# The second down projection of a hybrid decoder block: 16 of its 22 chunks as 2x2 blocks with seven block products

## The chip, the cores and the metric

The kernel runs on one core of a Trainium2 chip. TensorE (PE) multiplies, with its weight loads shown apart as PEld; VectorE (DVE), ScalarE (ACT) and GpSimd (POOL) do the element-wise work; SyncE (SP) and ACT issue DMAs. SBUF tiles have 128 partitions, results of PE land in eight PSUM banks of 128x512 float32. The metric is the device time of one execution in microseconds, as the median of several runs.

## The reference

A decoder block: a feed-forward layer, a mixer, and a second feed-forward layer, each between RMS norms, over 512 tokens and 1024 features, in float32. The part that matters here is the second feed-forward layer and its boundary:

```python
def swiglu(x, w_gu, w_down):                      # w_down: 2816 x 1024
    g, u = jnp.split(x @ w_gu, 2, axis=-1)
    return (jax.nn.silu(g) * u) @ w_down
...
        f = swiglu(rms_norm(h, ffn2_pre_g[l]), ffn2_w_gu[l], ffn2_w_down[l])
        h = h + MACARON_SCALE * rms_norm(f, ffn2_post_g[l])
```

With 128 rows to a chunk, the 2816 hidden features (ff) are 22 chunks.

## The kernel before

Every float32 operand is split into a high part, rounded to the matmul's input format (a cast on ACT), and a low part, the remainder (a subtraction on DVE). `mm3` (L129) makes a product of two split operands from three matmuls: high by high, high by low, low by high.

The stages follow one another: gate and up of layer 1 (`f1`), its down projection, the mixer, gate and up of layer 2 (`f2`), its down projection, and the last boundary (`b3`). A stage's gate and up matmuls are made in two ways: the first few chunks straight, the rest as pairs `k` = 0 to 17 in `paired` (L294), where a 2x2 block product is made with seven block multiplications (`product(1..7)`), 256 token columns moving, 12 matmuls each. Its order is written out by hand in `period(k)` under `tc.manual_schedule()`: products 1 and 2 of pair k, 5 of k-1, 6 and 7 of k, 3 and 4 of k-1, with preparation of the next pair's weights between. ACT copies a bank aside (`snap`), DVE adds (`add`), and `finish` makes the activations.

The down projection is `token_out` (L427). For each of the 22 chunks `wget` hands out one 128x1024 weight chunk: SP loads it as `wraw` (512 KB), `wsplit` (L96) casts on ACT (L100) and subtracts on DVE (L101). The activations `f2p` are split by chunk into `f2ph` and `f2pl` (L240, L241). Then for 4 token tiles of 128 and 2 halves of 512 output features one `mm3` each accumulates into the eight banks `f2o`: 24 matmuls of 128x512 per chunk, 528 in all. The last `TAILS[2]` = 5 chunks are kept back and multiplied token tile by token tile, so that tile after tile becomes ready. Outside `manual_schedule` a scheduler orders the instructions of each engine.

When a token tile is ready, `post_norm` (L199) takes its two banks: `Square` with a sum on ACT (L205), a scaled multiplication by the gain on DVE (L206), the mean on DVE (L209), the power -0.5 on POOL (L167), then on DVE the residual sum (L215) and out by two DMAs (L217).

Of the kernel before, what the change touches and what calls it, by code (L numbers as in the profile page):

```python
# [8 lines left out]
F32 = mybir.dt.float32  # L9
# [27 lines left out]

@with_exitstack
def hybrid_block_kernel(ctx, tc, x, xt, g1, w_first, gains, gu1, gs1, dn1, w_x, w_gate, w_q, w_k, w_v, w_gl, w_ga, w_pl, w_pa,
                        w_o, gu2, gs2, dn2, vecs, bd, sinks, rope, mask, out):  # L40
    nc = tc.nc
    V, A, G, PE, SP = nc.vector, nc.scalar, nc.gpsimd, nc.tensor, nc.sync

# [25 lines left out]
    for gu, dn in ((gu1, dn1), (gu2, dn2)):  # L69
        worder += [gu[j, i] for j in range(gu.shape[0]) for i in range(2)]  # L70
        caps.append(len(worder))
        worder += [dn[c] for c in range(KF)]
        if gu is gu1:
            worder += [w_x[c] for c in range(4)] + [w_k[i] for i in range(2)] + [w_v[i] for i in range(2)]
            worder += [w_x[c] for c in range(4, 8)] + [w_q[i] for i in range(4)]
            worder += [w_gate[c] for c in range(8)] + [w_q[i] for i in range(4, 8)]
            worder += [w[c] for c in range(8) for w in (w_gl, w_pl)]
            worder += [w[c] for c in range(8) for w in (w_ga, w_pa)]
            worder += [w_o[c] for c in range(8)]
# [163 lines left out]
    def gate_up(u, name, first, fast, rs=None):  # L243
        ps = []
        sp = []

        def split(c):
            if c % 4 == 0:
                sp.append((b8(f"{name}ph{c // 4}", [P, 4, T], F32R), b8(f"{name}pl{c // 4}", [P, 4, T], F32R)))
            split_chunk(ps[c // 4], *sp[-1], c % 4)  # L250

        def chunk(c):
            if c + 2 < KF and c >= 2:
                split(c + 2)
            return sp[c // 4]

        def tail(j, bg, bu):
            if j % 4 == 0:
                ps.append(b8(f"{name}p{j // 4}", [P, 4, T]))
# [8 lines left out]
            V.scalar_tensor_tensor(out=ps[-1][:, j % 4, :], in0=s, scalar=0.5, in1=bu, op0=ALU.mult, op1=ALU.mult)  # L268
# [20 lines left out]
        paired(fast(), name, ps)  # L289
        for c in range(4):  # L290
            split(c)
        return chunk

    def paired(fast, name, ps):  # L294
# [61 lines left out]
        def finish(k):  # L356
# [3 lines left out]
            if k % 2 == 0:  # L360
                d["ta"], d["tb"] = t2(f"{name}ta{k}"), t2(f"{name}tb{k}")
                ta, tb = d["ta"], d["tb"]
                A.activation(ta[:, lo_], a[:, lo_], AF.Tanh, scale=0.5)
                A.activation(ta[:, hi_], X, AF.Tanh, scale=0.5)
                A.activation(tb, b, AF.Tanh, scale=-0.5)
                for o, z in ((ta[:, lo_], a[:, lo_]), (ta[:, hi_], X), (tb, b)):
                    V.scalar_tensor_tensor(out=o, in0=o, scalar=1.0, in1=z, op0=ALU.add, op1=ALU.mult)
            else:
                ta, tb = st[k - 1]["ta"], st[k - 1]["tb"]
                if j % 4 == 0:  # L370
                    ps.append(b8(f"{name}p{j // 4}", [P, 4, T]))
                pa, pb = ps[-1][:, j % 4, :], ps[-1][:, j % 4 + 1, :]
# [9 lines left out]
        def period(k):  # L382
# [518 lines left out]
    chunk2 = gate_up(u3, "f2", first_four, lambda: (gs2, blocks(u3, mv3)))  # L901
    g_post, _ = gain_pair(5, 1, "g_b3")
    token_out(chunk2, KF, boundary(hs2, ov, g_post, None, None, 0.5, "b3"), "f2", TAILS[2])
# [5 lines left out]
def _layout(inputs):  # L909
# [44 lines left out]
    a["dn2"] = c(f["ffn2_w_down"].reshape(KF, P, D))  # L954
# [39 lines left out]
```

## Time and profile before

| | |
|---|---|
| median of 3 runs | 1159.97 us (1159.75 to 1160.45) |
| the profiled execution, first to last instruction (span) | 1158.4 us |
| median less span | 1.6 us |
| busy: PE, PEld, DVE, ACT, POOL | 98%, 87%, 69%, 46%, 5% of the span |
| second down projection, first to last matmul start | 1028.46 to 1150.93 us of the span |

The profiled execution has no time of its own beside its span; what lies around the span is taken as the median less the span. A matmul's row shows its own length, and matmuls overlap, so what one costs in a row of them is the distance between two starts (the pitch). The same holds for DVE and ACT, whose instructions in a row also start before the one before has ended.

### The profile page before, as it was taken

The numbers are of one execution on the slowest core, as the hardware profiler recorded it, in microseconds if no ns is written. First come the engines' busy times: TensorE is split into PE (matmuls) and PEld (weight loads), VectorE is DVE, ScalarE is ACT, GpSimd is POOL, SyncE is SP. The second block draws the span as 40 slices with busy tenths as digits, with TensorE's granted clock in tenths as the row PEclk, the third lists the DMA queues.
The fourth block names the chain that finished last, engine by engine and source line by source line (L and its number), as shares of the span: only waits on it lengthen the run. The fifth ranks groups of instructions, "written<-read, shape, count | busy, mean of one in ns | idle before, by whom it ended". The sixth has DMA issues, their size and how long they took to land.

```text
span 1158.4 us, 16623 instructions
## 1 busy us (share of the span) xinstructions
PE 1132.6 (98%) x6680; PEld 1008.4 (87%) x6680; DVE 804.2 (69%) x1182; ACT 537.3 (46%) x924; POOL 57.4 (5%) x58
## 2 busy tenths in 40 slices
PE   7979999999999999999999999999999999999997
PEld 6769999998888988887888888888999999998886
DVE  6598898984415887999877562546769898874303
ACT  7334555553313667566555341425435454553301
POOL 1000000000001010113121000000000000000000
PEclk9999999999999999999999999999999999999999
DMA  9113333284213453622822340624223333274011
GB/s 362 45 66 110 110 110 108 81 297 151 79 54 116 177 139 116 184 72 58 246 84 89 125 163 20 208 83 147 72 74 109 105 101 100 80 272 158 7 37 72
DMA packets 40604, 138.61 MB, mean 120 GB/s; under 512 B 4944, under 2 KB 5072, under 8 KB 39888
## 3 DMA queue, kind: packets, MB, share of 16 engines
q1 hardware_dynamic: 35920, 122.35, 32.4%
q10 hardware_dynamic: 4608, 15.21, 3.7%
q8 instruction: 52, 0.85, 0.3%
q14 instruction: 24, 0.20, 0.1%
HBM read 126.01 MB, written 11.53 MB: 119 GB/s over the span
## 4 chain that ended last, share of the span: by engine, by line
PE 87%; DVE 9%; ACT 2%; issue 2%; DMA 1%; POOL 0%; DVEq 0%; POOLq 0%; ACTq 0%
PE f1o L130 3%; PE f2o L130 3%; PE f1o L132 3%; PE f2o L132 3%; PE f1o L131 3%; PE f2o L131 3%; PE f2X L131 3%; PE f2X L132 3%; PE f2X L130 3%; PE f1X L130 3%; PE f1X L132 3%; PE f1X L131 3%; PE f1f L574 2%; PE f2Q L132 1%; PE f2Q L131 1%
## 5 line engine op out<-in xcount | busy, mean ns | idle before, releaser
L101 DVE TENSOR_TENSOR w<-wraw,w 128x1024 fp32r<-128x1024 f32 x128 | 155.7, 1244 | 67.0 <-ACT w L100 65.6
L100 ACT CAST w<-wraw 128x1024 fp32r<-128x1024 f32 x128 | 129.3, 1049 | 99.7 <-PE f1o L132 17.7
L130 PE MATMUL f1X<-u1m,f1W 128*128 128x256 f32 x256 | 73.1, 286 | 3.7 <-ACT f1sn L344 3.7
L132 PE MATMUL f1X<-u1m,f1W 128*128 128x256 f32 x256 | 73.2, 286 | 2.3 <-DVE f1W L324 2.3
L131 PE MATMUL f1X<-u1m,f1W 128*128 128x256 f32 x256 | 73.0, 285 | 0.0
L130 PE MATMUL f2o<-w,f2ph 128*128 128x512 f32 x176 | 68.6, 390 | 0.0
L130 PE MATMUL f1o<-w,f1ph 128*128 128x512 f32 x176 | 68.5, 390 | 0.0
L131 PE MATMUL f1o<-w,f1ph 128*128 128x512 f32 x176 | 68.5, 389 | 0.0
L131 PE MATMUL f2o<-w,f2ph 128*128 128x512 f32 x176 | 68.5, 389 | 0.0
L132 PE MATMUL f1o<-w,f1pl 128*128 128x512 f32 x176 | 67.0, 389 | 0.0
L132 PE MATMUL f2o<-w,f2pl 128*128 128x512 f32 x176 | 66.9, 389 | 0.0
L130 PEld LDWEIGHTS f1X<-u1m,f1W 128*128 128x128 f32 x256 | 49.6, 194 | 4.0 <-ACT f1sn L344 3.9
L132 PEld LDWEIGHTS f1X<-u1m,f1W 128*128 128x128 f32 x256 | 49.6, 194 | 2.6 <-DVE f1W L324 2.5
L131 PEld LDWEIGHTS f1X<-u1m,f1W 128*128 128x128 f32 x256 | 49.7, 194 | 0.1
L132 PE MATMUL f2X<-u3h,f2W 128*128 128x256 f32 x144 | 40.8, 283 | 0.0
L130 PE MATMUL f2X<-u3m,f2W 128*128 128x256 f32 x144 | 40.8, 283 | 0.0
L131 PE MATMUL f2X<-u3m,f2W 128*128 128x256 f32 x144 | 40.8, 283 | 0.0
L130 PE MATMUL f2Q<-u3m,f2W 128*128 128x256 f32 x144 | 40.8, 283 | 0.0
L131 PE MATMUL f2Q<-u3m,f2W 128*128 128x256 f32 x144 | 40.8, 283 | 0.0
L132 PE MATMUL f2Q<-u3m,f2W 128*128 128x256 f32 x144 | 40.8, 283 | 0.0
L131 PE MATMUL f2X<-u3l,f2W 128*128 128x256 f32 x144 | 40.8, 283 | 0.0
L132 PE MATMUL f2X<-u3m,f2W 128*128 128x256 f32 x144 | 40.7, 283 | 0.0
(722 smaller groups left out, 3519.9 us busy)
## 6 DMA issues: line engine op xcount, KB each, us to landing
wraw<-in_dn_dram SPq DMA_DIRECT2D x44, 512.0 KB, 4.7
f2L<-in_gs_dram SPq DMA_DIRECT2D x18, 512.0 KB, 3.6
f2R<-in_gs_dram SPq DMA_DIRECT2D x18, 512.0 KB, 4.4
wraw<-in_gu_dram SPq DMA_DIRECT2D x16, 512.0 KB, 5.8
f1L<-in_gs_dram SPq DMA_DIRECT2D x16, 512.0 KB, 3.6
f1R<-in_gs_dram SPq DMA_DIRECT2D x16, 512.0 KB, 4.4
wraw<-in_w_x_dram SPq DMA_DIRECT2D x8, 512.0 KB, 4.5
wraw<-in_w_q_dram SPq DMA_DIRECT2D x8, 512.0 KB, 4.4
```

Of the source, the lines that this page charges most:

```text
L100: A.copy(w[:, 0, :], raws[n])
L101: V.tensor_tensor(out=w[:, 1, :], in0=raws[n], in1=w[:, 0, :].bitcast(F32), op=ALU.subtract)
L130: PE.matmul(o, lhsT=ah, rhs=bh, start=start, stop=False, skip_group_check=reopen)
L131: PE.matmul(o, lhsT=ah, rhs=bl, start=False, stop=False, skip_group_check=reopen)
L132: PE.matmul(o, lhsT=al, rhs=bh, start=False, stop=stop, skip_group_check=reopen)
L574: PE.matmul(bs[i], lhsT=lw[:, i * P:(i + 1) * P], rhs=rx, start=k == 0 and n == 0, stop=k == KD - 1 and n == 2)
```

## The change

Chunks 0 to 15 of the second down projection become two groups (g = 0, 1) of 2x2 blocks. In a group the 512 tokens are two halves of 256, the ff features are two sets of four chunks (`GC`), and the 1024 outputs are two halves of 512. The four products of blocks of each output half become seven: the operands of a product are a block, or sums and differences of blocks, of the activations (token side) and of the weights. The weights of these chunks are laid out by quarter in a new input `ds2`.

A step is one product i, group g and half h of its contraction: 2 chunks x 2 token tiles x one `mm3`, 12 matmuls of 128x512. There are 7 x 2 x 2 = 28 steps, 336 matmuls, in the order of `PRODUCTS`. Chunks 16 to 21 are multiplied as before, 24 matmuls each, onto the same banks (144 matmuls). In all there are 480 matmuls in place of 528. `TAILS` for this stage goes from 5 to 4. The diff, cut to its core:

```diff
-TAILS = (6, 7, 5)
+TAILS = (6, 7, 4)
+GC = 4
+NS = 4 * GC
+LEAD = 3
+PRODUCTS = (1, 2, 5, 6, 3, 7, 4)
...
         for i in range(2):
-            A.activation(junk[:, cols[i]], banks[i], AF.Square, scale=1.0 / 32.0, accum_out=ms2[:, i:i + 1])
-            V.scalar_tensor_tensor(out=h[:, cols[i]], in0=banks[i], scalar=scale, in1=g[:, cols[i]],
+            z = banks[i]
+            if fix[i] is not None:
+                z = t2(f"{name}z{t}{i}")
+                V.tensor_tensor(out=z, in0=banks[i], in1=fix[i][0], op=fix[i][1])
+            A.activation(junk[:, cols[i]], z, AF.Square, scale=1.0 / 32.0, accum_out=ms2[:, i:i + 1])
+            V.scalar_tensor_tensor(out=h[:, cols[i]], in0=z, scalar=scale, in1=g[:, cols[i]],
                                    op0=ALU.mult, op1=ALU.mult)
...
         with tc.manual_schedule():
             for k in range(n):
                 period(k)
-        period(n)
-        add(n - 1, 21)
-        finish(n - 1)
+            if blocked is not None:
+                blocked.multiply(0)
+                blocked.prep(2)
+                product(5, n - 1, False)
...
+                blocked.multiply(1)
+                blocked.prep(3)
+                product(3, n - 1, False)
+                product(4, n - 1, False)
+                blocked.run(last, split_next)
...
+        def add_up(self, q):
...
+            if h == 0 and i in (5, 6, 3, 7):
...
+                V.tensor_tensor(out=o, in0=x0, in1=x1, op=ALU.subtract)
+            if i == 5:
+                z = self.raw[1, g, h]
+                V.tensor_tensor(out=z, in0=z, in1=self.raw[5, g, h], op=ALU.add)
+            if i == 7:
+                z = self.raw[5, g, h]
+                V.tensor_tensor(out=z, in0=z, in1=self.raw[3, g, h], op=ALU.add)
+
+        def prep(self, q):
+            self.load(q + 5)
+            self.add_up(q + 1)
...
+            w = b8(f"{self.name}w{i}{g}{h}", [P, 2, 2, 512], F32R)
+            A.copy(w[:, 0], z)
+            V.tensor_tensor(out=w[:, 1], in0=z, in1=w[:, 0].bitcast(F32), op=ALU.subtract)
+            self.w[i, g, h] = w
+            if i in (5, 6):
+                G.dma_start(first, self.ds[g, 3 if i == 5 else 2, h], accum_op=ALU.add)
...
+        def run(self, last, split_next):
+            for q in range(2, len(self.steps)):
+                if q == 3:
+                    last()
+                self.prep(q + LEAD - 1)
+                self.multiply(q)
+                for at_, key, of in ((6, "s1", "X"), (14, "s5", "Z"), (18, "s2", "X"), (26, "s3", "X")):
+                    if q == at_:
+                        self.snap(key, of)
+                if q == 20:
+                    open_loader()
+                if q in (23, 25, 26, 27):
+                    split_next()
```

`prep` makes a step's operands: for h = 0 the token operand `a` (cast on ACT, subtraction on DVE, both 128x1024), and for each h the weight operand `w` (the same). SP's `load` brings in 16 weight quarters of 512 KB; two more quarters per group and half are added to the one in SBUF by eight DMAs from POOL's queue with `accum_op`. `multiply(q)` is issued after the operands of the step two later. `multiply(0)` and `multiply(1)` stand between the last products of pair 17. The banks X, Y, Z and V, two each, hold the products; four copies (`snap`) keep values aside, and `post_norm` adds or subtracts one to each bank of a token tile.

On DVE, where the weights are prepared. Before, chunk weights `w` and the splits of the activations follow one another:

```order
L101 TENSOR_TENSOR w110_9940<-wraw110_9802,w110_9940 128x1024
L374 SCALAR_TENSOR_TENSOR f2p5_9854<-f2ta16_9806,f2X17_9686 128x256
L241 TENSOR_TENSOR f2pl1_9946<-f2p1_7944,f2ph1_9945 128x512 x2
L354 TENSOR_TENSOR f2cb17_9728<-f2Q17_9688,f2sn17_9725 128x256
L241 TENSOR_TENSOR f2pl1_9946<-f2p1_7944,f2ph1_9945 128x512 x2
L374 SCALAR_TENSOR_TENSOR f2p5_9854<-f2tb16_9807,f2cb17_9728 128x512
L101 TENSOR_TENSOR w111_9973<-wraw111_9877,w111_9973 128x1024
L101 TENSOR_TENSOR w112_10004<-wraw112_9914,w112_10004 128x1024
L101 TENSOR_TENSOR w113_10035<-wraw113_9943,w113_10035 128x1024
L101 TENSOR_TENSOR w114_10066<-wraw114_9976,w114_10066 128x1024
```

After, around the fifth product (`f2w21h`: weights of product 2, group 1; `f2b`: quarters as loaded; `f2sum`: differences of activations; `f2a`, `f2w`: low parts of a step's two operands):

```order
L535 TENSOR_TENSOR f2w210_9941<-f2b21_9774,f2w210_9941 128x1024
L505 TENSOR_TENSOR f2sum0_9958<-f2p0_7425,f2p1_7478 128x1024
L508 TENSOR_TENSOR f2b100_9682<-f2b100_9682,f2b50_9867 128x1024
L535 TENSOR_TENSOR f2w211_9961<-f2b21_9774,f2w211_9961 128x1024
L508 TENSOR_TENSOR f2b101_9684<-f2b101_9684,f2b50_9867 128x1024
L529 TENSOR_TENSOR f2a50_9977<-f2sum0_9958,f2a50_9977 128x1024
L535 TENSOR_TENSOR f2w500_9980<-f2b100_9682,f2w500_9980 128x1024
L505 TENSOR_TENSOR f2sum1_10000<-f2p8_8443,f2p9_8444 128x1024
L508 TENSOR_TENSOR f2b110_9686<-f2b110_9686,f2b51_9920 128x1024
L535 TENSOR_TENSOR f2w501_10003<-f2b101_9684,f2w501_10003 128x1024
L508 TENSOR_TENSOR f2b111_9688<-f2b111_9688,f2b51_9920 128x1024
L529 TENSOR_TENSOR f2a51_10020<-f2sum1_10000,f2a51_10020 128x1024
```

A quarter is added to another and an activation difference made before the low parts of the step: three instructions of 128x1024 for a step of product 5.

On ACT, in the period of the last pair (17). Before (`f2sn`, `f2sw`: banks copied aside; `f2W3`, `f2W4`: weights of pair 17; `w1xx`: the down projection's weights):

```order
L344 COPY f2sn17_9725<-f2X17_9686 128x256
L344 COPY f2sw16_9730<-f2X16_9577 128x256
L363 ACTIVATE f2ta16_9806<-f2ca16_9618 128x256
L344 COPY f2sn17_9725<-f2X17_9686 128x256
L323 CAST f2W317_9782<-f2L17_9436 128x1024
L323 CAST f2W417_9785<-f2N17_9569 128x512
L364 ACTIVATE f2ta16_9806<-f2X16_9577 128x256
L100 CAST w106_9794<-wraw106_9788 128x1024
L100 CAST w107_9799<-wraw107_9790 128x1024
```

After, casts of the first two steps and one of the third and their token operands stand among them:

```order
L524 ACTIVATE f2a10_9697<-f2p0_7425 128x1024
L534 CAST f2w100_9700<-f2b100_9682 128x1024
L365 COPY f2sn17_9742<-f2X17_9703 128x256
L365 COPY f2sw16_9747<-f2X16_9577 128x256
L534 CAST f2w101_9776<-f2b101_9684 128x1024
L365 COPY f2sn17_9742<-f2X17_9703 128x256
L344 CAST f2W317_9804<-f2L17_9436 128x1024
L344 CAST f2W417_9807<-f2N17_9569 128x512
L524 ACTIVATE f2a11_9825<-f2p8_8443 128x1024
L534 CAST f2w110_9828<-f2b110_9686 128x1024
L365 COPY f2sw17_9843<-f2X17_9703 128x256
```

The cast of `f2w100` now stands ahead of the copy `f2sn17`, which follows product 1 of pair 17.

On POOL, from the boundary ahead of layer 2 to the last one. Before:

```order
L167 TENSOR_TENSOR b2qpr3_7178<-b2qpe3_7176,mhalf_118 128x1
L167 TENSOR_TENSOR b2nr3_7186<-b2nme3_7184,mhalf_118 128x1
L167 TENSOR_TENSOR b3qpr0_10470<-b3qpe0_10468,mhalf_118 128x1
L167 TENSOR_TENSOR b3qpr1_10516<-b3qpe1_10514,mhalf_118 128x1
```

After, the eight accumulating DMAs stand between them, four for the fifth product's quarters and four for the sixth's:

```order
L172 TENSOR_TENSOR b2nr3_7186<-b2nme3_7184,mhalf_118 128x1
L538 DMA f2b100_9682<-in_ds2_dram 128x1024
L538 DMA f2b101_9684<-in_ds2_dram 128x1024
L538 DMA f2b110_9686<-in_ds2_dram 128x1024
L538 DMA f2b111_9688<-in_ds2_dram 128x1024
L538 DMA f2b100_9682<-in_ds2_dram 128x1024
L538 DMA f2b101_9684<-in_ds2_dram 128x1024
L538 DMA f2b110_9686<-in_ds2_dram 128x1024
L538 DMA f2b111_9688<-in_ds2_dram 128x1024
L172 TENSOR_TENSOR b3qpr0_10518<-b3qpe0_10516,mhalf_118 128x1
```

## Rows read from the trace of the kernel before

**Rows 1.** The page's first two parts: busy time in us, share of the span and number of instructions; and the granted clock of TensorE in 40 slices, in tenths.

```profile
span 1158.4 us, 16623 instructions
...
PE 1132.6 (98%) x6680; PEld 1008.4 (87%) x6680; DVE 804.2 (69%) x1182; ACT 537.3 (46%) x924; POOL 57.4 (5%) x58
...
PEclk9999999999999999999999999999999999999999
```

**Rows 2.** Busy time by stretch: eleven periods of pairs of gate and up of layer 2, up to the start of pair 17; the down projection ahead of its last tiles; its last tiles. Columns: us, then busy us and instructions of PE, PEld, DVE, ACT, POOL, then the granted clock, DMA share, GB/s.

```profile
906.60:1017.30 110.70, 110.70 (x925) 110.70 (x924) 99.77 (x154) 55.87 (x93) 0.00 (x0) 1.00 0.33 100
1040.00:1127.50 87.50, 87.50 (x388) 72.45 (x387) 29.74 (x33) 23.52 (x30) 0.00 (x0) 1.00 0.23 78
1127.50:1151.30 23.80, 23.80 (x106) 19.38 (x104) 9.45 (x16) 4.83 (x14) 1.65 (x3) 1.00 0.18 67
```

**Rows 3.** Timeline of PE near the end of the down projection: start, length, line, operation. The second row is the 27th matmul after the first, and the last of the kernel.

```profile
1144.81 0.39 PE L132 MATMUL f2o<-w,f2pl 128*128 128x512 f32 x1
...
1150.93 0.39 PE L132 MATMUL f2o<-w,f2pl 128*128 128x512 f32 x1
```

**Rows 4.** The stretch of the down projection again, only instructions that touch `f2o`: PE, PEld, DVE, ACT with their numbers.

```profile
1028.30:1151.30 123.00, 120.13 (x528) 98.97 (x528) 4.84 (x7) 4.83 (x14) 1.00 0.29 103
```

**Rows 5.** Timeline of PE: the first matmul of pair 16 and of pair 17 (84 matmuls apart).

```profile
1006.70 0.28 PE L130 MATMUL f2X<-u3h,f2W 128*128 128x256 f32 x1
...
1016.78 0.28 PE L130 MATMUL f2X<-u3h,f2W 128*128 128x256 f32 x1
```

**Rows 6.** Timeline of DVE, instructions that follow each other without a wait: 256, 1024, 1024 and 512 columns, and later 512 and three of 1024 in one row.

```profile
922.04 0.41 DVE L352 TENSOR_TENSOR f2cb<-f2Q,f2sw 128x256 f32<-128x256 f32 x1
922.38 1.21 DVE L324 TENSOR_TENSOR f2W<-f2M,f2W 128x1024 fp32r<-128x1024 f32 x1
923.51 1.22 DVE L324 TENSOR_TENSOR f2W<-f2L,f2W 128x1024 fp32r<-128x1024 f32 x1
924.64 0.68 DVE L324 TENSOR_TENSOR f2W<-f2N,f2W 128x512 fp32r<-128x512 f32 x1
...
1040.06 0.68 DVE L374 SCALAR_TENSOR_TENSOR f2p<-f2tb,f2cb 128x512 f32<-128x512 f32 x1
1040.66 3.49 DVE L101 TENSOR_TENSOR w<-wraw,w 128x1024 fp32r<-128x1024 f32 x3
```

**Rows 7.** Timeline of ACT: the copy aside of pair 17's first product, with the idle time before it, and three casts of 128x1024 in one row.

```profile
1018.42 0.37 ACT L344 COPY f2sn<-f2X 128x256 f32<-128x256 f32 x1 [3.92 <-PE f2X L132]
...
1038.75 2.95 ACT L100 CAST w<-wraw 128x1024 fp32r<-128x1024 f32 x3
```

**Rows 8.** Timeline of the end, after the last matmul.

```profile
1151.36 0.60 ACT L205 ACTIVATE b3qsq<-f2o 128x512 f32<-128x512 f32 x1 [2.71 <-PE f2o L132]
1151.85 0.19 ACT L205 ACTIVATION_READ_ACCUMULATOR b3qsq<-f2o 128x1 f32 x1
1152.08 0.69 DVE L206 SCALAR_TENSOR_TENSOR b3rh<-f2o,g_b 128x512 f32<-128x512 f32 x1 [2.71 <-ACT b3qsq L205]
1152.69 0.20 DVE L209 TENSOR_SCALAR b3qpe<-b3qps 128x1 f32<-128x1 f32 x1
...
1153.62 1.42 DVE L215 SCALAR_TENSOR_TENSOR b3rh<-b3rh,b3qpr 128x512 f32<-128x512 f32 x2 [0.73 <-POOL b3qpr L167]
```

**Rows 9.** Timeline of POOL and DVE, two places in the mixer where both work, and one where POOL does not.

```profile
549.30 1.29 POOL L710 TENSOR_TENSOR q2m<-q2m,q2m 128x512 f32<-128x512 f32 x1
549.50 1.11 DVE L770 TENSOR_TENSOR at13ss<-at13ss,at13e 128x4 f32<-128x4 f32 x1 [0.93 <-ACT at13s L768]
...
593.15 1.90 POOL L772 TENSOR_TENSOR at21s<-at21s,at21ss 128x1024 f32<-128x1024 f32 x1 [3.46 <-issue]
593.43 2.70 DVE L101 TENSOR_TENSOR w<-wraw,w 128x1024 fp32r<-128x1024 f32 x1 [0.41 <-ACT w L100]
...
617.49 0.16 DVE L770 TENSOR_TENSOR at22ss<-at22ss,at22e 128x4 f32<-128x4 f32 x1 [0.42 <-ACT at22s L768]
```

**Rows 10.** DMAs of 512 KB: SP's first issues for the down projection (time of the first, eight issues in the row); all 22 of them with the time of the issuing instruction and the min/median/max to landing; and the loads of x at the kernel's start, KB each and median us to landing.

```profile
1005.39 23.59 SPq L93 DMA_DIRECT2D wraw<-in_dn_dram  x8
...
L93 SPq DMA_DIRECT2D wraw<-in_dn_dram x22: 327/328/606, 1005.4 to 1069.3; - x22
DMA to landing us min/median/max: 3.3/4.5/7.6
...
x<-in_x_dram SPq DMA_DIRECT2D x4, 512.0 KB, 8.4
```

More of the change, by code (lines that the diff above doesn't have):

```diff
@@ L39, in hybrid_block_kernel @@
 def hybrid_block_kernel(ctx, tc, x, xt, g1, w_first, gains, gu1, gs1, dn1, w_x, w_gate, w_q, w_k, w_v, w_gl, w_ga, w_pl, w_pa,
-                        w_o, gu2, gs2, dn2, vecs, bd, sinks, rope, mask, out):
+                        w_o, gu2, gs2, dn2, ds2, vecs, bd, sinks, rope, mask, out):
     nc = tc.nc
@@ L71, in hybrid_block_kernel @@
         caps.append(len(worder))
-        worder += [dn[c] for c in range(KF)]
+        worder += [dn[c] for c in range(dn.shape[0])]
         if gu is gu1:
@@ L197, in to_features, with post_norm @@
                 A.copy(raw[half][:, :, ts_], bv)
-    def post_norm(banks, t, g, rh, scale, name, dst=None):
+    def post_norm(banks, fix, t, g, rh, scale, name, dst=None):
         ms2 = sm(f"{name}ps{t}", 2)
@@ L241, in split_chunk, with gate_up, pw @@
         V.tensor_tensor(out=pl[:, i, :], in0=p[:, i, :], in1=ph[:, i, :].bitcast(F32), op=ALU.subtract)
-    def gate_up(u, name, first, fast, rs=None):
-        ps = []
+    def gate_up(u, name, first, fast, rs=None, ds=None):
+        ps = {}
         sp = []
+        base = NS if ds is not None else 0
+        def pw(j):
+            if j < base:
+                key, slot, n = (j // (2 * GC), j % 2), j // 2 % GC, GC
+            else:
+                key, slot, n = (j - base) // 4, (j - base) % 4, 4
+            if key not in ps:
+                ps[key] = b8(f"{name}p{j}", [P, n, T])
+            return ps[key][:, slot, :]
         def split(c):
-            if c % 4 == 0:
-                sp.append((b8(f"{name}ph{c // 4}", [P, 4, T], F32R), b8(f"{name}pl{c // 4}", [P, 4, T], F32R)))
-            split_chunk(ps[c // 4], *sp[-1], c % 4)
+            i = c - base
+            if i % 4 == 0:
+                sp.append((b8(f"{name}ph{i // 4}", [P, 4, T], F32R), b8(f"{name}pl{i // 4}", [P, 4, T], F32R)))
+            split_chunk(ps[i // 4], *sp[-1], i % 4)
         def chunk(c):
-            if c + 2 < KF and c >= 2:
+            if c + 2 < KF and c >= base + 2:
                 split(c + 2)
-            return sp[c // 4]
+            return sp[(c - base) // 4]
         def tail(j, bg, bu):
-            if j % 4 == 0:
-                ps.append(b8(f"{name}p{j // 4}", [P, 4, T]))
             s = t2(f"{name}s{j}")
@@ L267, in tail @@
             V.scalar_tensor_tensor(out=s, in0=s, scalar=1.0, in1=bg, op0=ALU.add, op1=ALU.mult)
-            V.scalar_tensor_tensor(out=ps[-1][:, j % 4, :], in0=s, scalar=0.5, in1=bu, op0=ALU.mult, op1=ALU.mult)
+            V.scalar_tensor_tensor(out=pw(j), in0=s, scalar=0.5, in1=bu, op0=ALU.mult, op1=ALU.mult)
         bs = []
@@ L288, in gate_up, with paired @@
             tick()
[L289 to L294, printed above, removed]
+        blocked = None if ds is None else Blocked(name, ps, ds)
+        ahead = iter(range(base, base + 4))
+        paired(fast(), name, pw, blocked, lambda: split(next(ahead)))
+        if blocked is None:
+            for c in range(4):
+                split(c)
+        return chunk, blocked
+    def paired(fast, name, pw, blocked, split_next):
         src, mv = fast
@@ L389, in period @@
                 parts(d, 1)
+            elif blocked is not None:
+                blocked.prep(0)
             if c:
@@ L406, in period @@
                     parts(d, 2)
+                elif blocked is not None:
+                    blocked.prep(1)
                 snap(k, "s2")
@@ L413, in period, with last @@
                 parts(k, 4)
-            if k == n - 1:
-                wcap[0] = caps[caps.index(wcap[0]) + 1]
-                wload(wpos[0] + RAHEAD)
+            if k == n - 1 and blocked is None:
+                open_loader()
                 wsplit(wpos[0] + AHEAD)
+            if blocked is not None and k == n - 2:
+                for q in range(5):
+                    blocked.load(q)
             load(k + 3)
+        def last():
+            add(n - 1, 21)
+            finish(n - 1)
         with tc.manual_schedule():
@@ L428, in token_out, with open_loader @@
+    def open_loader():
+        wcap[0] = caps[caps.index(wcap[0]) + 1]
+        wload(wpos[0] + RAHEAD)
+    def token_out(chunk, n, epilogue, name, tail_n, blocked=None):
         banks = {}
+        base = NS if blocked is not None else 0
         def block(t, c, w, half):
@@ L432, in block @@
             ts_ = slice(t * P, (t + 1) * P)
+            opened = None if blocked is None else blocked.opened(t, half)
             if (t, half) not in banks:
-                banks[t, half] = bank(f"{name}o{t}{half}")
+                banks[t, half] = bank(f"{name}o{t}{half}") if opened is None else opened
             ns = slice(half * 512, (half + 1) * 512)
-            mm3(banks[t, half], ph[:, c % 4, ts_], pl[:, c % 4, ts_], w[0][:, ns], w[1][:, ns], c == 0, c == n - 1)
+            mm3(banks[t, half], ph[:, (c - base) % 4, ts_], pl[:, (c - base) % 4, ts_], w[0][:, ns], w[1][:, ns],
+                c == base and opened is None, c == n - 1, opened is not None)
         chunks = {}
         tail = []
-        for c in range(n):
+        for c in range(base, n):
             w = wget()
@@ L453, in token_out @@
                     block(t, c, w, half)
-            start(epilogue(t, (banks[t, 0], banks[t, 1])))
+            fix = [None, None] if blocked is None else [blocked.correction(t, half) for half in range(2)]
+            start(epilogue(t, (banks[t, 0], banks[t, 1]), fix))
             tick()
@@ L468, in boundary, with epilogue @@
         residual()
-        def epilogue(t, banks):
+        def epilogue(t, banks, fix):
             residual()
-            h = post_norm(banks, t, g_post, rhs[t], scale, f"{name}q", dst[t] if g_pre is None else None)
+            h = post_norm(banks, fix, t, g_post, rhs[t], scale, f"{name}q", dst[t] if g_pre is None else None)
             if g_pre is None:
@@ L899, in hybrid_block_kernel @@
                                                   lambda: moving(raw3, "u3", mv3)), "wo", TAILS[1])
[L901 removed]
+    chunk2, blocked2 = gate_up(u3, "f2", first_four, lambda: (gs2, blocks(u3, mv3)), None, ds2)
     g_post, _ = gain_pair(5, 1, "g_b3")
[L903 removed]
+    token_out(chunk2, KF, boundary(hs2, ov, g_post, None, None, 0.5, "b3"), "f2", TAILS[2], blocked2)
 _VECS = ["conv_b", "lru_b_a", "lru_b_x", "lru_lambda"]
@@ L953, in _layout, with quarters @@
     a["gu2"], a["gs2"] = gu(f["ffn2_w_gu"])[:JSTD["f2"]], pairs_of(f["ffn2_w_gu"], JSTD["f2"])
-    a["dn2"] = c(f["ffn2_w_down"].reshape(KF, P, D))
+    a["dn2"] = c(f["ffn2_w_down"].reshape(KF, P, D)[NS:])
+    def quarters(w):
+        b = w[:NS * P].reshape(2, 2, 2, 2, P, 2, 512)
+        return c(b.transpose(0, 5, 3, 1, 4, 2, 6).reshape(2, 2, 2, 2, P, 1024))
+    q = quarters(f["ffn2_w_down"])
+    a["ds2"] = c(np.stack([q[:, 0, 0], q[:, 1, 0], q[:, 0, 1], q[:, 1, 1]], 1))
     vec = [f["conv_w"][i] for i in range(4)] + [f[n] for n in _VECS]
```

87 lines of the change are left out of this document (82 added, 5 removed).

## The prediction

> **What bounds the kernel now.** I read the page's first parts, then busy time by stretch, then timelines at both ends of the changed stage. PE is busy for 98% of the span, at nine tenths of its full clock or more in each slice [rows 1]. Over the down projection ahead of its last tiles PE is busy for 87.50 of 87.50 us, DVE for 29.74, ACT for 23.52 [rows 2]: PE alone sets the pace there, and the other two have room. In the pairs before it DVE is nearly full too, 99.77 of 110.70 us [rows 2]; a preparation that reaches back into the last pair finds little room there. A matmul costs its pitch: from 1144.81 to 1150.93 are 27 of them, 0.2267 us each [rows 3]. A 256-column matmul costs 0.12 us, from 84 in 10.08 us [rows 5].
>
> The stage closes to the microsecond. Pair 17 ends its own period at 1016.78 + 10.08 = 1026.86. Its products 5, 3 and 4 are 36 matmuls, 4.32 us; 528 matmuls [rows 4] are 119.70; together 1150.88. The last one really starts at 1150.93 and so ends its turn at 1151.16 [rows 3]: 0.28 us of gaps in 124 us.
>
> **Matmuls.** 336 + 144 = 480 in place of 528, of the same shape. 48 x 0.2267 = **10.88 us** less, if PE still never waits. Nothing hides this, as PE is the bound; what hides a wait must be shown step by step.
>
> **When PE needs what.** multiply(0) runs from 1026.86, a step takes 12 x 0.2267 = 2.72 us, product 5 of the pair 1.44, multiply(1) follows, then 2.88 us of products 3 and 4. Step q from 2 on starts at S(q) = 1036.62 + 2.72 x (q - 2): S(10) = 1058.4, S(12) = 1063.8, S(14) = 1069.3, S(15) = 1072.0, S(22) = 1091.0, S(27) = 1104.6.
>
> **DVE in the blocks.** By the code the operations of 128x1024 per product are 6 for products 1, 2 and 4 (2 low parts of `a`, 4 of `w`), 8 for 6 and 3 (two differences more), 12 for 5 and 7 (four weight additions more): 58. One costs 1.13 us of pitch (922.38, 923.51, 924.64; and three in 3.49 less an overlap), 512 columns 0.60, 256 columns 0.34 [rows 6]. 58 x 1.135 = 65.8 us against 28 x 2.72 = 76.2 of PE: enough on the whole, but not in products 5 and 7, with 13.6 us of DVE beside 10.9 of PE. So the lead must last. DVE last waits for the pair's product 5: that ends at 1031.0, ACT's copy takes 0.37 like the one in [rows 7], so DVE goes on at about 1031.7. From there to the low part of step 10 the order has 18 operations of 1024 columns (20.4 us) and 3.5 us of small ones of the last pair (seven of 256 columns, two of 512): 1055.6. PE wants it at 1058.4: a lead of 2.8 us, the smallest. To step 22 are 28 more, 31.8 us: 1087.4 against 1091.0, lead 3.6. Cost: **0**; the cover is DVE's lead, and whatever takes more than 2.8 us from DVE before step 10, or 3.6 before step 22, shows on PE one for one.
>
> **ACT.** 42 casts at 0.98 (three in 2.95) [rows 7] are 41 us of 76, and eight copies of banks at about 0.6. Each copy of a bank stands behind casts that run with DVE's work, two to six steps ahead of the matmul that overwrites it; its cover is the same lead. 0.
>
> **DMA.** SP loads 16 + 6 pieces of 512 KB where it loaded 22; eight more come over POOL's queue: 30 against 22, in a stretch where the DMA engines are 23% busy [rows 2]. 0 for SP's. For the eight accumulating ones the trace has no row. A plain 512 KB takes 3.3 to 7.6 us to landing, 8.4 in the crowd at the start [rows 10]. The tightest is the third: it can start when step 10's low part is made (1055.6) and must have landed a cast (1.0) and a subtraction (1.22) before S(14): 1069.3 - 2.3 - 1055.6 = 11.4 us. I take the middle of the nearest row, 4.5 us, so 0. Bounds: 3.3 (0 as well) and twice the slowest, 15.2, an estimate for a transfer that also reads its target: 3.8 us.
> The Trainium skill ("DMA: Bandwidth & Descriptors", section "Anatomy of one DMA — SWDGE (gpsimd) path") fits a GpSimd-issued DMA as 2.0 us plus bytes over 436e3, an estimate of 3.2 us for 512 KB; no run here shows an accumulating one, and by that figure the sum would be the same.
>
> **The end.** The last bank is first corrected by DVE (0.69, the length of its neighbour in [rows 8]), then ACT squares it while DVE multiplies. Before, Square began at 1151.36, its sum ended at 1152.04, DVE's multiplication ran after it and the mean began at 1152.69 [rows 8]: 1.33 us. Now 0.69 + about 0.1 to pass it on + 0.68 for Square and its sum = 1.5, DVE beside it: **+0.15**, bounds -0.1 (the pass free, DVE's mean at once) and +0.69 (nothing overlaps). Per tile DVE has two corrections (1.3), two multiplications (1.3), the mean and the last sum (1.42): 4.2 us, under 24 x 0.2267 = 5.44 that a tile now takes on PE, so earlier tiles are not late.
>
> **Sum.** -10.88 + 0.15 = -10.73. The span goes from 1158.4 to 1147.7; the profiled run's time has 1.6 us around the span, taken as unchanged, so against the median 1159.97 the forecast is **1149.2**. Own range 1148.2 (no gap left, the low end bound) to 1150.5 (the high bound and half a microsecond of waits at the hand-over of stages).
>
> **Rivals.**
> *B, POOL holds DVE.* While POOL worked on SBUF, a DVE subtraction of 1024 columns took 2.70 us, not 1.22, and a tiny one 1.11, not 0.16 [rows 9]: 1.48 and 0.95 lost. DVE's operations in the blocks have two SBUF inputs, and POOL issues eight DMAs beside them. If making each one holds DVE as long, DVE loses 7.6 to 11.8 us before step 22, of which 3.6 is covered: 1153.2 to 1157.4. Against: POOL's rows are computations on SBUF data, and DMA issues carry none. Chance 0.12.
> The Trainium skill ("SBUF — State Buffer", section "Who interferes with whom") says that a VectorE instruction with two SBUF inputs contends with a GpSimd instruction that reads SBUF, which these rows bear out with 1.48 us; it infers that building DMA descriptors needs the write interface only, by which this rival would fall away.
> *C, the accumulates land late.* At 15.2 us each, side by side: 15.2 - 11.4 = 3.8 us: 1153.0. For: they read and write their target. Against: the engines are 23% busy. 0.09.
> *D, they go one after another, and it is slower.* Each waits for the one before, R apiece. The fourth, started in turn from step 8's low part (1055.6 less six operations = 1048.8), must land by S(15) - 2.3 = 1069.7: loss 4R - 20.9; the eighth by S(27) - 2.3 = 1102.3: 8R - 53.5. At R = 7.6 the larger is 9.5 (1158.7); at 8.4 it is 13.7 (1162.9). Slower than before from R = 8.0 on. For: one queue, and a crowd did take 8.4 [rows 10]. Against: SP's issues, one queue too, land in 4.5 while several are under way. 0.09.
> *E, the hand-over in the last pair.* The cast of `f2w100` now stands on ACT ahead of the copy of pair 17's first product, which had to wait 3.92 us for PE at 1018.42 [rows 7]. The cast needs quarter 100, whose load stands where SP's first issue stood, 1005.39 [rows 10]; the copy must be done by 1021.2 (product 6 overwrites the bank). Even 8.4 us would do; a late buffer on top would cost PE 1 to 3 us: 1150 to 1153. 0.06.
> That the change doesn't do what it says is excluded: the order on PE has 48 rows fewer.
>
> **Numbers.** Forecast 0.64, B 0.12, C 0.09, D 0.09, E 0.06. A measurement can tell 0.2%, 2.3 us, from no change. Faster (under 1157.65): all but D and a little of B, 0.89. Within: the lower part of D and the top of B, 0.04. Slower (over 1162.3): the rest of D, 0.07. The range leaves out D and the upper half of B, about 0.15, and a little below: 1148.0 to 1155.5.
>
> **What would show it.** Right: matmuls on the blocks' banks in one unbroken row of 0.2267 us from 1027 to 1140, the last about 11.2 us earlier; DVE's step-10 low part some 3 us ahead of PE. B: DVE rows of 1024 columns over 1.3 us beside POOL's DMA rows. C or D: PE idle before products 6 or 4, with a POOL DMA as releaser, and its time to landing over 11 us, or growing from one to the next. E: PE idle near 1021. Wrong in the main term: a pitch of the block matmuls other than 0.2267.

## The result, and the profile after

The changed kernel takes 1150.09 us (median of 4 runs, 1149.67 to 1151.21), the kernel before beside it 1159.86; the ratio is 0.9918, 95% interval 0.9904 to 0.9932. The forecast was 1149.2. The span of the profiled execution goes from 1158.4 to 1147.9 us; the forecast's was 1147.7.

The page's parts that answer to [rows 1]:

```profile
span 1147.9 us, 16623 instructions
...
PE 1121.6 (98%) x6632; PEld 999.0 (87%) x6632; DVE 847.0 (74%) x1216; ACT 558.2 (49%) x942; POOL 64.4 (6%) x66
...
PEclk9999999999999999999999999999999999999999
```

There are 48 matmuls fewer (6632 against 6680), the share of PE is unchanged, and DVE's busy time is 43 us up. Two stretches of the changed stage, the blocks from step 2 on and the six straight chunks; columns as in [rows 2]:

```profile
1036.60:1107.30 70.70, 70.31 (x309) 57.63 (x308) 67.12 (x64) 45.79 (x53) 7.11 (x8) 1.00 0.63 176
1107.30:1140.30 33.00, 33.00 (x147) 27.35 (x146) 16.88 (x27) 4.79 (x13) 1.66 (x3) 1.00 0.13 48
```

In the blocks PE is busy for 70.31 of 70.70 us, and DVE for 67.12, 95%: it has become nearly as tight as PE. Before, DVE was busy for a third of the time there, and the DMA engines' share was 0.23, which is 0.63 now [rows 2]. One place shows that it was too tight, in the timeline of PE (start, length, line, operation, and in brackets the idle time before and what ended it); the last row is the kernel's last matmul:

```profile
1090.98 0.39 PE L135 MATMUL f2X<-f2w,f2a 128*128 128x512 f32 x1
1091.75 0.50 PE L136 MATMUL f2X<-f2w,f2a 128*128 128x512 f32 x1 [0.39 <-DVE f2w L535]
1092.09 0.39 PE L137 MATMUL f2X<-f2w,f2a 128*128 128x512 f32 x1
...
1140.40 0.39 PE L137 MATMUL f2X<-w,f2pl 128*128 128x512 f32 x1
```

Between 1090.98 and 1091.75 PE misses 0.54 us over its pitch, and the next start is late by 0.11 too: step 22 waited for a DVE instruction. With 0.19 at step 21 (its rows are not shown), PE loses 0.85 us by these rows. There is no other gap in the blocks. Why DVE was late stands in its own timeline, the low parts of steps 13, 14 and 15 and, in the last row, of steps 22 and 23:

```profile
1062.30 1.23 DVE L535 TENSOR_TENSOR f2w<-f2b,f2w 128x1024 fp32r<-128x1024 f32 x1 [0.65 <-ACT f2w L534]
...
1066.19 1.22 DVE L535 TENSOR_TENSOR f2w<-f2b,f2w 128x1024 fp32r<-128x1024 f32 x1 [1.53 <-ACT f2w L534]
...
1069.89 1.23 DVE L535 TENSOR_TENSOR f2w<-f2b,f2w 128x1024 fp32r<-128x1024 f32 x1 [1.33 <-ACT f2w L534]
...
1090.48 2.35 DVE L535 TENSOR_TENSOR f2w<-f2b,f2w 128x1024 fp32r<-128x1024 f32 x2
```

DVE stood idle 0.65 + 1.53 + 1.33 = 3.51 us, each time until ACT had cast a weight quarter. ACT in turn waited for a DMA. The view of the line with the accumulating DMAs (operation, number, length of the issue; who waited for them; time to landing):

```profile
L538 POOL DMA_DIRECT2D f2b<-in_ds_dram x8: 863/866/1033, 1049.7 to 1071.4; - x8
...
  ACT f2w L534: 6.7, 3
...
DMA to landing us min/median/max: 5.7/9.8/10.5
```

They landed in 5.7 to 10.5 us, 9.8 in the median, where I had taken 4.5.

A ledger from the start of multiply(0) (1026.52 in the trace after) to the start of the last matmul: if PE never waits it is 36 x 0.12 + 479 x 0.2267 = 112.91 us; the changed kernel took 113.88. The kernel before took 124.07 by the same measure (1026.86 to 1150.93). So 11.2 us were to be had, its 0.28 us of gaps among them, and 10.2 came. The last pair began 0.34 us earlier in this execution (1016.44 against 1016.78 in [rows 5]); multiply(0) starts between 1025.64 and 1028.33 us in the traces that follow, so below everything is measured from there. Each kernel of the experiments but the last two was run once.

### The profile page after: what moved, and what is told of

It is laid out like the page before. It is cut to its first block, busy times and chain, and to the rows that moved or that the text cites. A ratio compares the mean times of both kernels' runs of the same rounds, so it can differ in the third digit from the quotient of the medians.

```text
span 1147.9 us, 16623 instructions
## 1 busy us (share of the span) xinstructions
PE 1121.6 (98%) x6632; PEld 999.0 (87%) x6632; DVE 847.0 (74%) x1216; ACT 558.2 (49%) x942; POOL 64.4 (6%) x66
## 4 chain that ended last, share of the span: by engine, by line
PE 85%; DVE 10%; ACT 2%; issue 2%; DMA 1%; POOL 0%; DVEq 0%; POOLq 0%; ACTq 0%
PE f2X L136 4%; PE f2X L137 4%; PE f2X L135 4%; PE f1o L135 3%; PE f1o L137 3%; PE f1o L136 3%; PE f1X L135 3%; PE f1X L137 3%; PE f1X L136 3%; PE f1f L736 2%; PE f2Q L137 2%; PE f2Q L136 2%; PE f2Q L135 2%; DVE w L106 1%; PE f1Q L135 1%
## 5 line engine op out<-in xcount | busy, mean ns | idle before, releaser
L106 DVE TENSOR_TENSOR w<-wraw,w 128x1024 fp32r<-128x1024 f32 x112 | 136.4, 1248 | 44.8 <-ACT w L105 43.4
L105 ACT CAST w<-wraw 128x1024 fp32r<-128x1024 f32 x112 | 112.9, 1049 | 64.8 <-PE f1o L137 17.7
L135 PE MATMUL f1o<-w,f1ph 128*128 128x512 f32 x176 | 68.5, 390 | 0.0
L136 PE MATMUL f1o<-w,f1ph 128*128 128x512 f32 x176 | 68.5, 389 | 0.0
L137 PE MATMUL f2X<-u3h,f2W 128*128 128x256 f32 x144 | 40.8, 283 | 0.0
L135 PE MATMUL f2X<-u3h,f2W 128*128 128x256 f32 x144 | 40.7, 283 | 0.0
L135 PEld LDWEIGHTS f1o<-w,f1ph 128*128 128x128 f32 x176 | 33.0, 188 | 6.9 <-ACT f1ph L249 0.2
L136 PEld LDWEIGHTS f1o<-w,f1ph 128*128 128x128 f32 x176 | 33.0, 188 | 6.9
```

The lines of the kernel that those rows point to most:

```text
L105: A.copy(w[:, 0, :], raws[n])
L106: V.tensor_tensor(out=w[:, 1, :], in0=raws[n], in1=w[:, 0, :].bitcast(F32), op=ALU.subtract)
L135: PE.matmul(o, lhsT=ah, rhs=bh, start=start, stop=False, skip_group_check=reopen)
L136: PE.matmul(o, lhsT=ah, rhs=bl, start=False, stop=False, skip_group_check=reopen)
L137: PE.matmul(o, lhsT=al, rhs=bh, start=False, stop=stop, skip_group_check=reopen)
```

## The experiments

Two theories stood against each other. Theory 1: the accumulating DMAs land late, DVE, which works in order, stands idle for them, and has no lead left when product 7 needs twelve of its instructions. Theory 2: product 7's twelve instructions alone do it. Inside theory 1: is it the addition that makes the DMAs slow (1a), or POOL's queue and the crowd of other loads (1b)? Waits of under 0.1 us are not counted as idle. In the table a lead is the start of a step's first matmul less the end of its weights' low part; idle is DVE's before steps 13 to 15.

| | multiply(0) to last matmul | DVE idle | lead at step 10, 15, 22 | accumulates, median to landing |
|---|---|---|---|---|
| changed kernel | 113.88 us | 3.51 us | 2.2, 0.6, -0.7 | 9.8 us |
| no_accumulate | 112.96 | 0 | 2.2, 4.2, 2.5 | none |
| plain_from_pool | 112.96 | 0 | 2.2, 4.1, 2.4 | 4.9 (plain) |
| late_chunk_loads | 112.97 | 0.95 | 2.2, 3.1, 1.5 | 7.9 |
| early_adds | 112.96 | 0.27 | 2.2, 0.6, 2.3 | 9.7 |
| four_more_dve | 118.76 | 3.52 | 2.2, 0.6, (PE waits) | 9.7 |

**no_accumulate.**

```diff
-            if i in (5, 6):
-                G.dma_start(first, self.ds[g, 3 if i == 5 else 2, h], accum_op=ALU.add)
```

> Leaves out the eight accumulating DMAs, so products 6 and 4 use weight sums that lack a quarter. In the changed kernel DVE stood idle 3.51 us before the low parts of steps 13, 14 and 15, and PE then waited 0.85 us at product 7 (0.19 at step 21, 0.66 at step 22). Theory 1, the accumulates land late (9.8 us median) and eat DVE's lead: DVE's three idle places vanish, the lead at step 22 goes from -0.67 to about +2.8 us, PE has no gap in the blocks, and the span is 0.8 to 0.9 us shorter, 1147.0. Theory 2, product 7's twelve DVE instructions alone use up the lead: the gap at step 22 stays, 0.5 us or more. If DMA issues on POOL held DVE, DVE's pitch of 1.135 us would fall in this run; I expect the same pitch.

Span 1146.4 us. DVE never stood idle, and PE had no gap. DVE's timeline at the low parts of steps 22 and 23 (one row, L535), and PE's where step 22 begins (1090.30):

```profile
1086.55 2.35 DVE L535 TENSOR_TENSOR f2w<-f2b,f2w 128x1024 fp32r<-128x1024 f32 x2
1088.82 1.21 DVE L529 TENSOR_TENSOR f2a<-f2p,f2a 128x1024 fp32r<-128x1024 f32 x1
```

```profile
1090.08 0.39 PE L137 MATMUL f2X<-f2w,f2a 128*128 128x512 f32 x1
1090.30 0.39 PE L135 MATMUL f2X<-f2w,f2a 128*128 128x512 f32 x1
1090.53 0.39 PE L136 MATMUL f2X<-f2w,f2a 128*128 128x512 f32 x1
```

The low part of step 22 was done at 1087.8 (1086.55 and a length of 1.21), 2.5 us ahead of PE. Theory 2 falls: product 7 takes its lead from DVE, but has enough if nothing was lost before. The span fell by more than the gap, since this execution also reached multiply(0) 0.4 us earlier.

**plain_from_pool.**

```diff
-                G.dma_start(first, self.ds[g, 3 if i == 5 else 2, h], accum_op=ALU.add)
+                G.dma_start(first, self.ds[g, 3 if i == 5 else 2, h])
```

> The same eight DMAs from POOL's queue without the addition: the quarter in SBUF is overwritten, so products 6 and 4 use wrong sums; instructions, order and waits are those of the changed kernel. Theory 1a, the addition itself is what takes long (it reads and writes its target): time to landing falls from 9.8 us median to 4 to 6, DVE's idle 3.51 us and PE's 0.85 us vanish. Theory 1b, POOL's queue or the crowd of other loads makes them slow: landing stays at 8 to 10 us and DVE still waits over 2 us.

Span 1146.4 us. The line's view, and the part of the DMA view from 1048 to 1080 us that shows POOL's queue (packets, MB, share of 16 engines):

```profile
L538 POOL DMA_DIRECT2D f2b<-in_ds_dram x8: 537/537/747, 1049.1 to 1067.4; - x8
...
DMA to landing us min/median/max: 4.0/4.9/7.4
```

```profile
q0 software_dynamic: 1152, 4.19, 38.6%
```

For the changed kernel the same share reads:

```profile
q0 software_dynamic: 1150, 4.19, 68.5%
```

The same queue, waits and bytes without the addition land in 4.9 us instead of 9.8, and take 38.6% of the DMA engines' time where the addition takes 68.5%. So the addition itself is the larger cause (1a). POOL's row of one DMA is shorter too, 0.54 us against 0.87.

**late_chunk_loads.**

```diff
...
-        wload(wpos[0] + RAHEAD)
+        wload(wpos[0] + RAHEAD, A if wcap[0] == len(worder) else None)
```

The part that is left out hands the queue on to `wload`.

> The three first loads of the straight chunks' weights are issued from ACT's queue, behind the cast for step 22, in place of SP's queue, where they ran from 1053.8 on beside the accumulates. Theory 1b, the crowd slows the accumulates: landing falls from 9.8 to 7 to 8.5 us median, DVE's idle falls from 3.51 to under 2 us, PE's gap at step 22 falls under 0.3 us. Theory 1a, the addition itself sets the pace: landing within 0.7 us of 9.8, DVE idle over 2.5 us, PE's gap over 0.5 us.

Span 1146.1 us. The accumulates' landing from the line's view, and in DVE's timeline the two idle places that were left:

```profile
DMA to landing us min/median/max: 6.0/7.9/8.5
```

```profile
1061.39 1.23 DVE L535 TENSOR_TENSOR f2w<-f2b,f2w 128x1024 fp32r<-128x1024 f32 x1 [0.63 <-ACT f2w L534]
...
1064.07 1.23 DVE L535 TENSOR_TENSOR f2w<-f2b,f2w 128x1024 fp32r<-128x1024 f32 x1 [0.32 <-ACT f2w L534]
```

The landing fell to 7.9 us, and that was enough: no gap on PE. So 1a's number for this run was wrong. Both causes are there: of the 4.9 us between a plain and an accumulating DMA in the changed kernel, about 2 go with the loads beside it, which were issued from 1053.8 us on and first cast at 1097.2.

Why both count can be read from the DMA engines' time in the same 32 us. SP's loads (q1) in the changed kernel and in plain_from_pool, and both queues in this run:

```profile
q1 hardware_dynamic: 989, 3.59, 30.1%
...
q1 hardware_dynamic: 1013, 3.66, 31.8%
...
q0 software_dynamic: 1152, 4.19, 68.6%
q1 hardware_dynamic: 542, 1.96, 18.5%
```

With the rows of q0 above, the two queues kept the 16 engines busy for 98.6% in the changed kernel, 87.1% here and 70.4% with plain DMAs, and the median landing falls in that order: 9.8, 7.9, 4.9 us. By an estimate from these rows an accumulating DMA takes all engines for 2.74 us (68.5% of 32 us, over eight), a plain one for 1.54; one was issued every 3.1 us (eight starts within 21.7 us). So in the changed kernel the engines were full. That the DMAs waited for one another there fits these numbers; no run tests it by itself.

**four_more_dve.**

```diff
             V.tensor_tensor(out=w[:, 1], in0=z, in1=w[:, 0].bitcast(F32), op=ALU.subtract)
+            if i == 3:
+                V.tensor_tensor(out=w[:, 1], in0=z, in1=w[:, 0].bitcast(F32), op=ALU.subtract)
```

> The low part of the weights is computed twice in the four steps of product 3: four more DVE instructions of 128x1024, 4.54 us. The prediction said that beyond the lead DVE's time shows on PE one for one. DVE enters step 16 with a lead of 1.05 us, so: PE waits about 4.54 + 0.85 = 5.4 us in products 3 and 7 together in place of 0.85, and the span grows by 4.5 us, to 1152.4. Rival, DVE only touched the bound and PE's order absorbs more (snaps and weight loads ahead): span grows by under 2.5 us.

Span 1152.5 us. PE at two places in product 3:

```profile
1077.05 0.39 PE L135 MATMUL f2Z<-f2w,f2a 128*128 128x512 f32 x1
1077.95 0.50 PE L136 MATMUL f2Z<-f2w,f2a 128*128 128x512 f32 x1 [0.51 <-DVE f2w L537]
...
1081.47 0.50 PE L136 MATMUL f2Z<-f2w,f2a 128*128 128x512 f32 x1 [0.47 <-DVE f2w L537]
```

PE waited 118.76 - 112.96 = 5.80 us in all, against 0.92 in the changed kernel: 4.88 more, where 4.54 was expected. DVE was late by as much: from multiply(0) to the end of step 22's low part it took 70.06 us, against 65.18 in the changed kernel, 4.88 more. So one for one holds. The four instructions cost more than their pitch of 1.135, as one of the doubled pairs shows (L537 writes the tile of L535 again):

```profile
1075.41 1.22 DVE L535 TENSOR_TENSOR f2w<-f2b,f2w 128x1024 fp32r<-128x1024 f32 x1
1076.66 1.23 DVE L537 TENSOR_TENSOR f2w<-f2b,f2w 128x1024 fp32r<-128x1024 f32 x1
```

The second starts 1.25 us after the first, in all four steps. Of these 5.0 us 0.1 came back at the token operand's low part behind them, which had waited for ACT in the changed kernel.

**early_adds.** The four weight additions for product 7 stand ahead of steps 13, 14, 15 and 17.

```diff
-            if i == 7:
+            early = {14: 16, 15: 17, 16: 18, 18: 19}
+            if q in early:
+                i, g, h = self.steps[early[q]]
                 z = self.raw[5, g, h]
                 V.tensor_tensor(out=z, in0=z, in1=self.raw[3, g, h], op=ALU.add)
```

> The four additions of weight quarters for product 7 are moved ahead on DVE, three to the places where it stood idle (ahead of the low parts of steps 13, 14 and 15) and one ahead of step 17's; the loads stay as they were. Theory 1: the accumulates still land in 9 to 10.5 us, the three idle places shrink from 3.51 us to under 0.6 because additions fill them, leads at steps 14 and 15 stay small (0.5 to 1.6 us), the lead at step 22 goes from -0.67 to between +2.2 and +3 us, and PE has no gap of over 0.1 us in the blocks. Rival, the place that decides is not step 22 but the late landing at step 15 itself: a new gap of 0.3 us or more at steps 14 to 17.

Span 1146.2 us. DVE around the low parts of step 13 (1061.94) and step 15 (1069.16), with the moved additions in L513:

```profile
1060.80 1.22 DVE L513 TENSOR_TENSOR f2b<-f2b,f2b 128x1024 f32<-128x1024 f32 x1
1061.94 1.22 DVE L537 TENSOR_TENSOR f2w<-f2b,f2w 128x1024 fp32r<-128x1024 f32 x1
1063.08 1.22 DVE L513 TENSOR_TENSOR f2b<-f2b,f2b 128x1024 f32<-128x1024 f32 x1
...
1067.67 1.22 DVE L513 TENSOR_TENSOR f2b<-f2b,f2b 128x1024 f32<-128x1024 f32 x1
1069.16 1.23 DVE L537 TENSOR_TENSOR f2w<-f2b,f2w 128x1024 fp32r<-128x1024 f32 x1 [0.27 <-ACT f2w L536]
```

The accumulates were as late as ever (9.7 us), and the lead at step 15 as small; but DVE did its additions in that time, and the lead at step 22 was 2.3. Here the lateness cost PE nothing; what cost in the changed kernel is that DVE had nothing to do in it.

**no_correction.**

```diff
-            fix = [None, None] if blocked is None else [blocked.correction(t, half) for half in range(2)]
+            fix = [None, None]
```

> Leaves out the correction of each bank by its side copy in the last boundary, so the output lacks these terms. The changed kernel took 1.91 us from the start of the last matmul to the mean (1140.40 to 1142.31), the kernel before 1.76 (1150.93 to 1152.69). By the prediction's step the correction costs 0.15 us: without it 1.76 us again. Rival, it costs its own length and only the other tiles hide it: under 1.4 us, or DVE's corrections hold back earlier tiles, and the last tile's chain shortens by over 0.4 us.

The end of this run, from the last matmul, and then that of the changed kernel, from its last correction on (its last matmul stands above, 1140.40):

```profile
1142.07 0.39 PE L137 MATMUL f2X<-w,f2pl 128*128 128x512 f32 x1
1142.50 0.60 ACT L214 ACTIVATE b3qsq<-f2X 128x512 f32<-128x512 f32 x1 [1.97 <-PE f2X L137]
...
1143.22 0.69 DVE L215 SCALAR_TENSOR_TENSOR b3rh<-f2X,g_b 128x512 f32<-128x512 f32 x1 [1.95 <-ACT b3qsq L214]
1143.83 0.20 DVE L218 TENSOR_SCALAR b3qpe<-b3qps 128x1 f32<-128x1 f32 x1
```

```profile
1140.83 0.69 DVE L213 TENSOR_TENSOR b3qz<-f2X,f2s 128x512 f32<-128x512 f32 x1 [0.33 <-PE f2X L137]
1141.55 0.63 ACT L214 ACTIVATE b3qsq<-b3qz 128x512 f32<-128x512 f32 x1 [0.97 <-DVE b3qz L213]
1141.55 0.69 DVE L215 SCALAR_TENSOR_TENSOR b3rh<-b3qz,g_b 128x512 f32<-128x512 f32 x1
...
1142.31 0.21 DVE L218 TENSOR_SCALAR b3qpe<-b3qps 128x1 f32<-128x1 f32 x1
```

1142.07 to 1143.83 is 1.76 us, as before the change; 1140.40 to 1142.31 is 1.91. The correction costs 0.15 us: `Square` (L214) and the multiplication (L215) both start at 1141.55, where they had run one after the other [rows 8]. This run's span, 1149.4, tells nothing of it: it reached multiply(0) 1.8 us later than the changed kernel, ahead of everything that the edit touches, and has the same gap at step 22.

**changed_again and late_loads_timed**: the changed kernel and the one of late_chunk_loads, four runs each on one chip, with seven of the kernel before.

> The changed kernel again, beside the next one, on one chip. A PE gap of 0.7 to 1.0 us at steps 21 and 22 as in the first profile, 3 to 4 us of DVE idle time before steps 13 to 15, and about 1150.1 us.

> The kernel with the straight chunks' first loads issued late from ACT's queue, timed. No gap on PE in the blocks; 0.85 us less than the changed kernel, 1149.2 us, which is the prediction's own sum; beside the kernel before a ratio near 0.991. A difference of 0.85 us is about as large as the runs of one kernel differ, so the trace from the last pair's start to the last matmul decides: 123.96 us in the changed kernel, 123.1 expected here.

The changed kernel took 1149.58 us (1149.47 to 1150.03), ratio 0.9912 (0.9897 to 0.9927); with the late loads it took 1148.95 (1148.49 to 1150.40), ratio 0.9909 (0.9892 to 0.9925); the kernel before 1159.75. In the traces: 113.72 us from multiply(0) to the last matmul with 0.65 us of gap at step 22 (a little under the 0.7 to 1.0 expected), against 112.96 without a gap. The medians differ by 0.63 us in that direction, but the intervals overlap: the gain of the late loads is shown by the traces, not by the times.

## Why the prediction was right, step by step

- **Matmuls, -10.88.** Right. Without a gap on PE four kernels took 112.96 or 112.97 us against 112.91 counted.
- **The end, +0.15.** Right: 1.91 against 1.76 us, and 1.76 again without the correction.
- **DVE's lead of 2.8 us at step 10 and 3.6 at step 22.** Too large: measured 2.2 at step 10 in every kernel, and 2.5 at step 22 in no_accumulate, where no DMA was waited for. The count of instructions held. At step 10 PE came 0.3 us earlier and DVE 0.3 later than worked out; from there to step 22 DVE took 32.3 us (1055.45 to 1087.76) and not 31.8, as four low parts of token operands (L529) started 0.07 to 0.15 us late, each right behind ACT's cast of the operand.
- **The accumulating DMAs, 0.** This term was mis-sized; the changed kernel lost 0.92 us by it. From multiply(0) to the last matmul the forecast comes to 124.07 - 10.88 = 113.19 us, which keeps the gaps of the kernel before, and 113.88 were measured: 0.69 over, most of the miss of the forecast (1150.09 against 1149.2). The rest is within what the runs of one kernel differ by (1149.67 to 1151.21). Two things in the term were off. The landing was taken as 4.5 us and was 9.8, inside the bounds of 3.3 and 15.2. And the limit of 11.4 us was worked out for PE alone. DVE came to the low part of step 13 at 1061.65, 8.9 us after the second accumulate was issued (1052.80). This DMA landed after 8.3 us, and DVE, which works in order, stood for 0.65, so a landing of more than about 7.7 us already stops it, and what it loses there is missing at step 22. The text had the rule, that whatever takes more than 3.6 us from DVE before step 22 shows on PE, and did not apply it to this wait. It would not have sufficed: 3.51 us of idle time are just under 3.6. With the lead of 2.54 that DVE really has, 0.97 is missing, and PE waited 0.92.
- **The range, 1148.2 to 1150.5.** It held 1150.09 in part by luck. Its high side stood for the end (+0.69) and for waits at the hand-over of stages, and neither came; the bound of the accumulating DMAs, 3.8 us, had been left to rival C.
- **B, POOL holds DVE.** Fell. DVE and POOL where the first two DMAs are issued:

```profile
1048.99 1.22 DVE L505 TENSOR_TENSOR f2sum<-f2p,f2p 128x1024 f32<-128x1024 f32 x1
1049.69 1.03 POOL L538 DMA_DIRECT2D f2b<-in_ds_dram  x1 [242.70 <-DVE f2w L535]
1050.13 1.22 DVE L508 TENSOR_TENSOR f2b<-f2b,f2b 128x1024 f32<-128x1024 f32 x1
1051.27 1.22 DVE L535 TENSOR_TENSOR f2w<-f2b,f2w 128x1024 fp32r<-128x1024 f32 x1
1052.40 1.22 DVE L508 TENSOR_TENSOR f2b<-f2b,f2b 128x1024 f32<-128x1024 f32 x1
1052.80 0.88 POOL L538 DMA_DIRECT2D f2b<-in_ds_dram  x1 [2.07 <-DVE f2w L535]
1053.54 1.22 DVE L529 TENSOR_TENSOR f2a<-f2sum,f2a 128x1024 fp32r<-128x1024 f32 x1
```

DVE's starts are 1.13 or 1.14 us apart with POOL's rows beside them, the pitch that they have without, where the rival took 0.95 to 1.48 us from each DMA. The lead at step 22 was 2.36 us with plain DMAs and 2.54 without any; this 0.18 us is no hold by POOL but one wait in plain_from_pool, for the third DMA, which landed at 1062.38. ACT casts its quarter, and step 14's low part starts 1.31 us after the instruction before it (1062.26):

```profile
1062.48 2.26 ACT L534 CAST f2w<-f2b 128x1024 fp32r<-128x1024 f32 x2 [0.25 <-DMA f2b<-in_ds_dram]
...
1063.57 1.23 DVE L535 TENSOR_TENSOR f2w<-f2b,f2w 128x1024 fp32r<-128x1024 f32 x1
```

The Trainium skill ("SBUF — State Buffer", section "Who interferes with whom") infers that building descriptors needs the write interface of the port pair that VectorE and GpSimd share, while a `tensor_tensor` takes only its read interface; these runs agree, with starts 1.13 to 1.14 us apart.
- **C, late accumulates.** The mechanism was this one; its size was 9.8 us and its way to PE led through DVE. The reason given against it, DMA engines 23% busy, was a share of the kernel before; while the accumulates ran the engines were full (98.6%). The Trainium skill ("DMA: Bandwidth & Descriptors", section "Anatomy of one DMA — SWDGE (gpsimd) path") fits a DMA issued from GpSimd as 2.0 us plus bytes over 436e3, an estimate of 3.2 us for this size. The traces decide: a plain one from POOL took 4.0 at the least and 4.9 in the median, an accumulating one 9.8, three times the estimate.
- **D, one after another.** Its price fell: the eight landed 3.7 us apart on average (1055.38 to 1081.14), where the rival took 7.6 to 8.4 for each. Part of its sign was there: in order of issue they landed after 5.7, 8.3, 8.8, 10.3 and 10.5 us, then 9.9, 9.8 and 9.7. So they seem to have queued, at a lower price.
- **E, the hand-over in the last pair.** Fell: PE ran unbroken from the pair's start at 1016.44 to multiply(0) at 1026.52, 10.08 us.

## What to carry to other kernels

When work moves from the engine that sets the pace to one that waits for it, write down the lead of that engine step by step, and subtract in it every wait of its own, not only the time its instructions take: here 3.5 us of idle time, seven to nine steps earlier, came out as 0.9 us on PE. Take the DMA engines' share from the stretch as it will be, not from the kernel before: here a transfer that adds cost them 1.8 times a plain one, and with the engines full it took twice as long to land. An idle place of an engine that works in order can be filled with work that is due later; moving four additions did as much here as a faster transfer. And a transfer that is not due for long need not run beside one that is.

## What the runs showed of the hardware that I had not expected

- A DMA of 512 KB that adds to its target took twice as long to land as a plain one from the same queue (9.8 against 4.9 us median), and 1.8 times the DMA engines' time (68.5% against 38.6% of the same 32 us).
- Issuing it took POOL 0.87 us, a plain one 0.54; DVE's starts beside it stayed 1.13 or 1.14 us apart.
- A DVE instruction that writes the tile of the one before it, as the doubled ones of four_more_dve do, started 1.25 us after it; the others in a row start 1.135 apart.
- After a wait PE's first matmul had a row of 0.50 us instead of 0.39, and the next start was 0.11 us late.
